# Feed-forward input of a decoder layer: the low part of every second weight tile by ACT and an accumulating DMA instead of DVE

## The chip, the core and the metric

The kernel runs on one core of a Trainium2 chip, as one launch. A core has five engines that run their own instruction queues: TensorE (PE) multiplies matrices from the on-chip memory into PSUM; VectorE (DVE), ScalarE (ACT) and GpSimd (POOL) work elementwise; SyncE (SP) here only issues DMAs. DMAs can be issued by SP, ACT or POOL, and are carried out by 16 DMA engines.

The metric is the device time of one execution in microseconds.

## What is computed

One layer of a decoder trunk on 256 tokens of 2048 features: a gated convolution branch and a block attention branch, merged and projected, then cross attention, then a gated feed-forward, each added to the residual stream, all in float32. The change is in the feed-forward input:

```python
def swiglu(h, w_in, w_out):
    g, u = jnp.split(h @ w_in, 2, axis=-1)
    return (jax.nn.silu(g) * u) @ w_out
...
    h = rmsnorm(x, norm_ffn_g[l])
    x = x + swiglu(h, w_ffn_in[l], w_ffn_out[l])
return rmsnorm(x, norm_final_g)
```

with `w_in` of 2048 x 11264 and `w_out` of 5632 x 2048.

## The kernel before

**Numbers in two parts.** TensorE gets its operands in the type float32r, which holds fewer bits than float32. To keep the precision, each operand is given as a high part (the value rounded to float32r) and a low part (the rest, value minus high part). A product then takes three matmuls into the same PSUM bank, in `mm3`: high x high (L116), high of the activations x low of the weights (L117), low x high (L118).

**The weight stream.** The whole layer is a list of blocks. A block is 1024 output columns (two ranges of 512) for both tiles of 128 tokens, over the whole contraction, in k-tiles of 128 rows. A k-tile is 128 x 1024 float32, 512 KB. Over all blocks, `stream` handles the k-tiles as one sequence with the running number q:

- `load_k` (L225) loads a k-tile into one of four `raw` buffers, from SP. In the feed-forward input the two column ranges lie apart, so that there are two DMAs, L233 and L234; in most other blocks it is one, L231.
- `split_k` (L237) makes the two parts, in one of four `whi` and one of four `wlo` buffers: ACT casts (`split`, L121), DVE subtracts (L122).
- `piece` (L258) issues the three matmuls for one token tile and one column range; a k-tile has four pieces, 12 matmuls of 512 columns.

**The order.** It is written out by the program itself, and every engine works through its own queue in that order. `ensure(q)` (L251) is called ahead of a k-tile's matmuls. It issues the splits up to tile q + 3, and ahead of each split of a tile s the loads up to tile s + 3. A buffer is taken over by the tile four numbers later: `whi` and `wlo` when TensorE has finished with them, `raw` when both the cast and the making of the low part have finished.

In the middle of a block the k-tiles are used one after the other. In its first and its last group, two k-tiles are used by turns, column range by column range (L285 to L299), and `ensure` is called once for both. At the end of a feed-forward block ACT applies SiLU (L846) and DVE multiplies (L849); the transposes of the result (L130, copied from PSUM by ACT on L133) stand among the first matmuls of the next block.

The feed-forward input is 11 blocks (`ffn_block`, L831) of 16 k-tiles. The output (`fo_block`, L875) follows it.

Of the kernel before, what the change touches and what calls it, by code (L numbers as in the profile page):

```python
# [12 lines left out]
ALU = mybir.AluOpType  # L13
# [3 lines left out]
P = 128  # L17
S = 256
D = 2048
KD = D // P  # L20
# [3 lines left out]
DFF = 5632  # L24
# [1 line left out]
EPS = 1e-6  # L26
NEG = -1e30

# columns of the packed per-partition vectors
C_MIX, C_MEM, C_CROSS, C_FFN = 0, 16, 32, 48  # L30
C_CW = 64
C_CB = C_CW + CC * TAPS
# [3 lines left out]


class Block:
    """One block of 1024 output columns for all 256 tokens: two 512-wide column
    ranges of a weight, both token tiles, the whole contraction."""  # L40

    def __init__(self, name, kt, lhs, cols, evac, before=None):
        self.name, self.kt, self.lhs, self.cols, self.evac = name, kt, lhs, cols, evac
        self.before = before


class Builder:
# [19 lines left out]
        self.ready = set()  # L67
        self.n = 0

# [1 line left out]
    def at(self, delay, fn, *args):  # L71
        heapq.heappush(self.tasks, (self.slot + delay, self.seq, fn, args))
        self.seq += 1

    def later(self, tr, n):
        """The transposes of a finished column range, a unit at a time."""
        for w in range(2):
            self.at(6 + 2 * n + 2 * w, tr, n, w)

# [31 lines left out]
        return bass.AP(tensor=src.tensor, offset=src.offset + off, ap=[[0, P], [1, n]])  # L111

    def mm3(self, out, lhs, rhs, start, stop):
        """out (+)= lhs.T @ rhs with each operand given as exact high and low parts."""
        mm = self.nc.tensor.matmul
        mm(out, lhs[0], rhs[0], start=start, stop=False)  # L116
        mm(out, lhs[0], rhs[1], start=False, stop=False)  # L117
        mm(out, lhs[1], rhs[0], start=False, stop=stop)  # L118
# [3 lines left out]
        self.nc.vector.tensor_tensor(lo, src, hi.bitcast(F32), op=ALU.subtract)  # L122

    def transposes(self, src, hi, lo, k, gain=None, mark=None):
        """Two k-tiles of both token tiles to [feature, token] and split."""
        nc = self.nc
        b = self.bank([P, 2, 2, P], "tr")
        for c in range(2):
            for t in range(2):
                nc.tensor.transpose(b[:, c, t, :], src(c, t), self.ident)  # L130
        bb = b.rearrange("p c t s -> p c (t s)")
        if lo is None:
            nc.scalar.copy(hi[:, k : k + 2, :], bb)  # L133
        elif gain is None:
            self.split(bb, hi[:, k : k + 2, :], lo[:, k : k + 2, :])
        else:
            for c in range(2):
                g = self.vecs[:, gain + k + c : gain + k + c + 1]
                nc.scalar.activation(hi[:, k + c, :], bb[:, c, :], AF.Copy, scale=g)
                nc.vector.scalar_tensor_tensor(  # L140
                    lo[:, k + c, :], bb[:, c, :], g, hi[:, k + c, :].bitcast(F32),
                    op0=ALU.mult, op1=ALU.subtract,
                )
        if mark:
            self.ready.update((mark, k + c) for c in range(2))
# [3 lines left out]
        self.nc.scalar.activation(j, src, AF.Square, accum_out=dst)  # L149

    def load_features(self, dst, src, k, n):
        """k-tiles of a [feature, token] array."""
        self.nc.sync.dma_start(dst[:, k : k + n, :], src[:, k : k + n, :])

    def split_gain(self, src, hi, lo, k, gain, mark):
        """Two k-tiles times their gains as high and low parts."""
        for i in (k, k + 1):
            g = self.vecs[:, gain + i : gain + i + 1]
            self.nc.scalar.activation(hi[:, i, :], src[:, i, :], AF.Copy, scale=g)
            self.nc.vector.scalar_tensor_tensor(  # L160
                lo[:, i, :], src[:, i, :], g, hi[:, i, :].bitcast(F32), op0=ALU.mult, op1=ALU.subtract
            )
            self.ready.add((mark, i))

    def feature_rstd(self, src, first, gap, done):
        """Reciprocal root mean square of every token of a [feature, token] tile: squares
        added over the k-tiles, then over the partitions; done(result) ends it."""
        acc = self.tok_tile([P, 2, S], "sqa")

        def square(u):  # L170
            s = self.tok_tile([P, 2, S], "sq") if u else acc
            self.nc.scalar.activation(s, src[:, 2 * u : 2 * u + 2, :], AF.Square)
            if u:
                self.nc.vector.tensor_tensor(acc, acc, s, op=ALU.add)

        def total():
            bk = self.bank([P, 2, 2], "ssq")
            for t in range(2):
                for c in range(2):
                    self.nc.tensor.matmul(bk[:, t, c : c + 1], acc[:, c, t * P : (t + 1) * P],  # L180
                                          self.ones[:, 0:1], start=True, stop=True)
            done(self.rstd_of(bk, "rf"))

        for u in range(8):
            self.at(first + gap * u, square, u)
        self.at(first + gap * 7 + 3, total)

    def rstd_of(self, ss, name):
        """[P, 2, n] partial sums of squares -> [P, 2] reciprocal root mean square."""
        nc = self.nc  # L190
        r = self.const.tile([P, 2], F32, name=self.nm(name))
        s = self.sm_tile([P, 2], "st")
        nc.vector.tensor_reduce(s, ss, axis=AX.X, op=ALU.add)
        q = self.sm_tile([P, 2], "sq")
        nc.scalar.activation(q, s, AF.Sqrt, bias=self.eps[:, 0:1], scale=1.0 / D)
        nc.vector.tensor_scalar(s, s, 1.0 / D, EPS, op0=ALU.mult, op1=ALU.add)
        nc.vector.reciprocal(r, q)
        nc.vector.tensor_tensor(s, s, r, op=ALU.mult)
        nc.vector.tensor_tensor(s, s, q, op=ALU.add)
        nc.vector.tensor_scalar_mul(s, s, 0.5)  # L200
        nc.vector.reciprocal(r, s)
        return r

# [1 line left out]
    def load_first(self):  # L205
        """The first two k-tiles, by halves in the order of their use."""
        for q in range(2):
            self.raw[q] = self.wts.tile([P, 2, 512], F32, tag="raw", name=self.nm("raw"))
        for j in range(2):
            for q in range(2):  # L210
                blk, k = self.kts[q]
                w, c = blk.cols[j]
                self.nc.sync.dma_start(self.raw[q][:, j, :], w[k * P : (k + 1) * P, c : c + 512])
# [23 lines left out]
    def split_k(self, q):  # L237
        r = self.raw.pop(q)
        hi = self.wts.tile([P, 2, 512], F32R, tag="whi", name=self.nm("whi"))
        lo = self.wts.tile([P, 2, 512], F32R, tag="wlo", name=self.nm("wlo"))  # L240
        self.split(r, hi, lo)
        self.w[q] = (hi, lo)

    def load_to(self, top):
# [71 lines left out]

        return f

# [1 line left out]
    def setup(self):  # L320
        nc, a = self.nc, self.a
        self.vecs = self.const.tile([P, NCOL], F32, name="vecs")
# [24 lines left out]
        )  # L347

    def col_tr(self, srcs, hi, lo, k, gain=None, mark=None):
        """Transposes of 256 columns from two token tiles' APs [P, 256]."""  # L350
        self.transposes(lambda c, t: srcs[t][:, c * P : (c + 1) * P], hi, lo, k, gain, mark)


# [4 lines left out]
def layer(ctx: ExitStack, tc: tile.TileContext, args, out):  # L358
# [3 lines left out]
    act, dve, pe = nc.scalar, nc.vector, nc.tensor  # L362
    b.setup()

    # ================= input norm (gain now, root mean square at evacuation) =========
    xin = b.big_tile([P, KD, S], F32, "xin")
    xh = b.big_tile([P, KD, S], F32R, "xh")
    xl = b.big_tile([P, KD, S], F32R, "xl")
# [9 lines left out]
        if q % 2 == 0 and q < 16:  # L378
            b.load_features(xin, a["x_t"], q, 2)

    # ================= input projection =================
    def bias_tile(hold, c0, c1):
        t = b.small.tile([P, 2, 512], F32, tag="bias", name=b.nm("bias"), bufs=2)
        nc.sync.dma_start(t[:, 0, :], b.bcast(a["b_in"], c0, 512))
# [48 lines left out]

        return Block(f"glu{j}", KD, b.lhs_of(xh, xl, "x"), [(a["w_in"], c0), (a["w_in"], c1)], evac, before)

    # taps per slot, alone and beside the block attention
    CONV_RATE, MOBA_RATE = 1.6, 0.6

    # causal depthwise convolution, one tap at a time, channels on partitions
    def conv_start():  # L440
        def tap(c, j):
            w = b.vecs[:, C_CW + c * TAPS + j : C_CW + c * TAPS + j + 1]
# [13 lines left out]
    ln = {}  # L456

    def tree(src, name):
        """Sum of eight [P, S] tiles."""
        s1 = b.tok_tile([P, 2, S], name)  # L460
        s2 = b.tok_tile([P, 2, S], name)
        dve.tensor_tensor(s1, src[:, 0:2, :], src[:, 2:4, :], op=ALU.add)
# [59 lines left out]
        if h == 0:  # L522
            b.at(2, ln_scale, 1)

    # keys, queries and values of the block attention
    def qk_block(name, col, which):
        hold = {}

# [88 lines left out]
        return Block(f"gate{which}{j}", KD, b.lhs_of(xh, xl, "x"),  # L617
                     [(a["w_in"], col), (a["w_in"], col + 512)], evac, before)

    # ================= merge and output projection =================  # L620
    tiles = {}

    def conv_out_block(j):
# [42 lines left out]
        return f  # L666

    def residual_block(name, w, j, kt, lhs, ssname, nxt, gain, mark, before=None):
        """x += block; sums of squares; transposed and split for the next product."""

        def evac(t, n, ps):
            c = j * 1024 + n * 512
# [21 lines left out]
        tiles["x2"] = [b.big_tile([P, KD, S], F32R, "x2") for _ in range(2)]  # L694
        tiles["ss2"] = b.const.tile([P, 2, 4], F32, name="ss2")

    # ================= cross attention =================
    def cq_block(j):
        hold = {}

# [126 lines left out]
        tiles["x3"] = [b.big_tile([P, KD, S], F32R, "x3") for _ in range(2)]  # L827
        tiles["ss3"] = b.const.tile([P, 2, 4], F32, name="ss3")

    # ================= gated feed-forward =================  # L830
    def ffn_block(j):  # L831
        hold = {}

# [24 lines left out]
            b.ready.update((("mid", k), ("mid", k + 1)))  # L858

        w = a["w_ffn_in"]  # L860
        return Block(f"ffn{j}", KD, lhs_t("x3", "x3"), [(w, 512 * j), (w, DFF + 512 * j)], evac, before)

    mids = {}

    def mid_split(j, k):
        """[P, 2, S] of the gated activations as high and low parts, ahead of use."""
        assert ("mid", k) in b.ready and ("mid", k + 1) in b.ready
        hi = b.tok_tile([P, 2, S], "mh", F32R)
        lo = b.tok_tile([P, 2, S], "ml", F32R)
# [33 lines left out]
        return Block(f"fo{j}", KF, lhs, [(w, j * 1024), (w, j * 1024 + 512)], evac, before)  # L903

    def part(t):
        """Mean square of the columns that are done, and the guard."""
        s = b.sm_tile([P, 1], "fst")
        dve.reduce_sum(s, tiles["ss4"][:, t, 0:3], axis=AX.X)
        dve.tensor_scalar(s, s, 1.0 / D, EPS, op0=ALU.mult, op1=ALU.add)
# [13 lines left out]
                dve.tensor_scalar_mul(o[:, cs], o[:, cs], q)  # L923
            (act if c == 1 else nc.sync).dma_start(rows[:, cs], o[:, cs])

    # ================= the order of the work =================
    def start():
        x_unit(0)
        for u in range(1, 8):
# [73 lines left out]
```

## Time and profile before

| | |
|---|---|
| time, median of 2 runs | 1726.76 us (1726.74 to 1726.79) |
| the profiled execution, first to last instruction | 1725.3 us |
| PE busy | 1714.2 us |
| DVE busy | 1034.3 us |
| ACT busy | 826.0 us |
| POOL busy | 1.6 us, 12 instructions |
| DMA traffic | 330.28 MB, mean 191 GB/s |
| feed-forward input, 985 to 1475 us | PE 490.0, ACT 215.5, DVE 234.9 us busy |

The profiled execution and the timed runs differ by 1.5 us, the work around the first and last instruction. Busy times are those of instructions that compute; the issue of a DMA is not counted, and stands on its own rows ("SPq" for SP's queue). A busy PE is not a PE at its peak, since matmuls are pipelined: a 512-column matmul is listed with 0.39 us, while they start 0.23 us apart. "Landing" is the time from a DMA's issue to its completion. In lists of groups, an arrow with a name after the idle time says what ended it.

### The profile page before, as it was taken

How to read it: one execution, taken by the hardware profiler on the slowest of the kernel's cores; microseconds unless marked ns; L12 is line 12 of the kernel's file. 1: busy time of each engine (PE TensorE's matmuls, PEld its weight loads, DVE VectorE, ACT ScalarE, POOL GpSimd, SP SyncE). 2: the span in 40 equal slices, each digit the busy share in tenths (PEclk: the TensorE clock that was granted, in tenths of full speed). 3: DMA queues.
4: the chain of work that ended last, by engine and by line, in shares of the span. 5: the costliest groups of instructions: out<-in, count | busy, mean ns of one | idle time of the engine just before them, and what ended most of it. 6: DMA issues, size and time to landing. Idle time of an engine off the chain costs nothing.

```text
span 1725.3 us, 20943 instructions
## 1 busy us (share of the span) xinstructions
PE 1714.2 (99%) x7830; PEld 1423.0 (82%) x7830; DVE 1034.3 (60%) x1265; ACT 826.0 (48%) x1020; POOL 1.6 (0%) x12
## 2 busy tenths in 40 slices
PE   9999999999999999999999999999999999999998
PEld 7888888888888888888888888888888888888886
DVE  6579987797765557445554554444444444555655
ACT  6544445544544556445444454444444444544543
POOL 0000000000000000000000000000000000000000
PEclk9999999999999999999999999999999999999999
DMA  8666665555665575554445555665656565655553
GB/s 297 197 205 196 195 196 172 187 191 186 208 226 181 187 244 184 184 186 155 136 158 189 184 190 191 195 195 185 193 185 193 185 194 185 216 195 193 192 193 133
DMA packets 122757, 330.28 MB, mean 191 GB/s; under 512 B 13600, under 2 KB 13728, under 8 KB 122528
## 3 DMA queue, kind: packets, MB, share of 16 engines
q1 hardware_dynamic: 122224, 328.26, 59.0%
q8 instruction: 61, 1.00, 0.2%
q10 hardware_dynamic: 432, 0.70, 0.1%
q14 instruction: 40, 0.33, 0.1%
HBM read 326.80 MB, written 2.10 MB: 191 GB/s over the span
## 4 chain that ended last, share of the span: by engine, by line
PE 99%; DMA 0%; DVE 0%; ACT 0%; DVEq 0%; issue 0%
PE acc L116 32%; PE acc L117 32%; PE acc L118 32%; PE tr L130 2%; DMA vecs<-in_vecs 0%; PE cb L118 0%; PE cs L116 0%; PE cs L118 0%; PE cs L117 0%; PE cb L117 0%; PE cb L116 0%; PE ms L570 0%; PE mo L597 0%; PE mt L589 0%; DVE wlo L122 0%; PE mo L598 0%
## 5 line engine op out<-in xcount | busy, mean ns | idle before, releaser
L122 DVE TENSOR_TENSOR wlo<-raw,whi 128x1024 fp32r<-128x1024 f32 (+1 forms) x602 | 727.7, 1220 | 563.8 <-ACT whi L121 563.0
L121 ACT CAST whi<-raw 128x1024 fp32r<-128x1024 f32 (+1 forms) x602 | 624.1, 1050 | 612.3 <-PE acc L118 525.4
L116 PE MATMUL acc<-whi,x 128*128 128x512 f32 x832 | 326.9, 393 | 0.0
L118 PE MATMUL acc<-whi,x 128*128 128x512 f32 x832 | 324.1, 390 | 0.0
L117 PE MATMUL acc<-wlo,x 128*128 128x512 f32 x832 | 323.9, 389 | 0.0
L116 PE MATMUL acc<-whi,xh 128*128 128x512 f32 x576 | 228.8, 397 | 1.0 <-ACT whi L121 1.0
L117 PE MATMUL acc<-wlo,xh 128*128 128x512 f32 x576 | 224.5, 390 | 0.2 <-DVE wlo L122 0.2
L118 PE MATMUL acc<-whi,xl 128*128 128x512 f32 x576 | 224.6, 390 | 0.0
L118 PEld LDWEIGHTS acc<-whi,x 128*128 128x128 f32 x832 | 156.2, 188 | 33.0
L117 PEld LDWEIGHTS acc<-wlo,x 128*128 128x128 f32 x832 | 156.3, 188 | 31.4
L116 PEld LDWEIGHTS acc<-whi,x 128*128 128x128 f32 x832 | 156.2, 188 | 31.4
L117 PE MATMUL acc<-wlo,mh 128*128 128x512 f32 x352 | 137.1, 389 | 0.1
L116 PE MATMUL acc<-whi,mh 128*128 128x512 f32 x352 | 137.1, 390 | 0.0
L118 PE MATMUL acc<-whi,ml 128*128 128x512 f32 x352 | 137.0, 389 | 0.0
L118 PEld LDWEIGHTS acc<-whi,xl 128*128 128x128 f32 x576 | 108.1, 188 | 23.0
L116 PEld LDWEIGHTS acc<-whi,xh 128*128 128x128 f32 x576 | 108.2, 188 | 22.7 <-ACT whi L121 1.2
L117 PEld LDWEIGHTS acc<-wlo,xh 128*128 128x128 f32 x576 | 108.3, 188 | 22.2 <-DVE wlo L122 0.8
L447 DVE SCALAR_TENSOR_TENSOR vy<-vt,vecs,vy 128x256 f32<-128x256 f32 x240 | 103.7, 477 | 0.0
L116 PE MATMUL acc<-whi,m 128*128 128x512 f32 x256 | 101.3, 396 | 0.0
L118 PE MATMUL acc<-whi,m 128*128 128x512 f32 x256 | 99.8, 390 | 0.0
L117 PE MATMUL acc<-wlo,m 128*128 128x512 f32 x256 | 99.8, 390 | 0.0
L117 PEld LDWEIGHTS acc<-wlo,mh 128*128 128x128 f32 x352 | 66.1, 188 | 14.0 <-DVE wlo L122 0.6
(206 smaller groups left out, 1630.8 us busy)
## 6 DMA issues: line engine op xcount, KB each, us to landing
raw<-in_w_ffn_in SPq DMA_DIRECT2D x352, 256.0 KB, 3.0
raw<-in_w_in SPq DMA_DIRECT2D x112, 512.0 KB, 3.6
raw<-in_w_ffn_out SPq DMA_DIRECT2D x88, 512.0 KB, 3.6
raw<-in_w_ckv SPq DMA_DIRECT2D x64, 512.0 KB, 3.6
raw<-in_w_in SPq DMA_DIRECT2D x64, 256.0 KB, 4.0
raw<-in_w_out SPq DMA_DIRECT2D x32, 512.0 KB, 4.8
raw<-in_w_cq SPq DMA_DIRECT2D x32, 512.0 KB, 4.8
raw<-in_w_co SPq DMA_DIRECT2D x32, 512.0 KB, 4.6
```

The source lines that it names most:

```text
L116: mm(out, lhs[0], rhs[0], start=start, stop=False)
L117: mm(out, lhs[0], rhs[1], start=False, stop=False)
L118: mm(out, lhs[1], rhs[0], start=False, stop=stop)
L121: self.nc.scalar.copy(hi, src)
L122: self.nc.vector.tensor_tensor(lo, src, hi.bitcast(F32), op=ALU.subtract)
L130: nc.tensor.transpose(b[:, c, t, :], src(c, t), self.ident)
L447: dve.scalar_tensor_tensor(y[:, c, :], src, w, y[:, c, :], op0=ALU.mult, op1=ALU.add)
```

## The change

The blocks of the feed-forward input get a mark, `by_dma`. For their odd k-tiles, the low part is made in another way: ACT writes the high part as before, then ACT writes the negated value into the low part's buffer, which rounds it to float32r and so gives minus the high part; then a DMA issued from POOL adds the raw tile to that buffer in place. The even k-tiles, and all other blocks, are split as before. Loads, buffers, the matmuls and their order are the same.

```diff
-    def __init__(self, name, kt, lhs, cols, evac, before=None):
+    def __init__(self, name, kt, lhs, cols, evac, before=None, by_dma=False):
         self.name, self.kt, self.lhs, self.cols, self.evac = name, kt, lhs, cols, evac
-        self.before = before
+        self.before, self.by_dma = before, by_dma
...
     def split_k(self, q):
         r = self.raw.pop(q)
         hi = self.wts.tile([P, 2, 512], F32R, tag="whi", name=self.nm("whi"))
         lo = self.wts.tile([P, 2, 512], F32R, tag="wlo", name=self.nm("wlo"))
-        self.split(r, hi, lo)
+        blk, k = self.kts[q]
+        if blk.by_dma and k % 2:
+            self.nc.scalar.copy(hi, r)
+            self.nc.scalar.mul(lo, r, -1.0)
+            self.nc.gpsimd.dma_start(lo, r, accum_op=ALU.add)
+        else:
+            self.split(r, hi, lo)
         self.w[q] = (hi, lo)
...
-        return Block(f"ffn{j}", KD, lhs_t("x3", "x3"), [(w, 512 * j), (w, DFF + 512 * j)], evac, before)
+        return Block(f"ffn{j}", KD, lhs_t("x3", "x3"), [(w, 512 * j), (w, DFF + 512 * j)], evac, before,
+                     by_dma=True)
```

The rest of the diff takes out comments and docstrings. Up to the loads (L231 to L234) the lines keep their numbers; the three new operations of the odd k-tiles stand on L243 (cast), L244 (negated copy) and L245 (accumulating DMA), and later lines move by six (SiLU from L846 to L852).

## The prediction

> **What bounds the kernel now.** I read the page's shares and its chain of waits first, then the window of the feed-forward input stage, then the timeline inside it, then the waits and the DMA landings.
>
> ```profile
> span 1725.3 us, 20943 instructions
> ...
> PE 1714.2 (99%) x7830; PEld 1423.0 (82%) x7830; DVE 1034.3 (60%) x1265; ACT 826.0 (48%) x1020; POOL 1.6 (0%) x12
> ...
> PE 99%; DMA 0%; DVE 0%; ACT 0%; DVEq 0%; issue 0%
> L122 DVE TENSOR_TENSOR wlo<-raw,whi 128x1024 fp32r<-128x1024 f32 (+1 forms) x602 | 727.7, 1220 | 563.8 <-ACT whi L121 563.0
> L121 ACT CAST whi<-raw 128x1024 fp32r<-128x1024 f32 (+1 forms) x602 | 624.1, 1050 | 612.3 <-PE acc L118 525.4
> ```
>
> The chain of waits is TensorE for 99% of the span: the program is one stream of matmuls. DVE and ACT are not busy enough to matter by themselves; both sit idle for more than 560 us ahead of these two groups, DVE until ACT's cast, and ACT mostly until TensorE gives a buffer back (L118).
>
> The window of the eleven feed-forward input blocks (columns: PE, PEld, DVE, ACT, POOL busy with counts, granted clock, DMA share, GB/s):
>
> ```profile
> 985.00:1475.00 490.00, 490.00 (x2208) 405.61 (x2207) 234.95 (x216) 215.50 (x235) 0.00 (x0) 1.00 0.60 190
> ```
>
> TensorE is busy for all of the 490 us, at full granted clock, while DVE is busy for 48% and ACT for 44%. So nothing can be won here by freeing DVE. What can be lost is decided by how much slack a weight k-tile has between its load and its first matmul. The timeline shows it: two ACT lines, one of DVE, three of SP's queue, all in mid block.
>
> ```profile
> 1043.20 1.05 ACT L121 CAST whi<-raw 128x1024 fp32r<-128x1024 f32 x1 [1.21 <-PE acc L118]
> 1045.92 1.05 ACT L121 CAST whi<-raw 128x1024 fp32r<-128x1024 f32 x1 [1.67 <-PE acc L118]
> ...
> 1044.29 1.22 DVE L122 TENSOR_TENSOR wlo<-raw,whi 128x1024 fp32r<-128x1024 f32 x1 [1.05 <-ACT whi L121]
> ...
> 1043.27 0.33 SPq L233 DMA_DIRECT2D raw<-in_w_ffn_in  x1
> 1043.64 0.43 SPq L234 DMA_DIRECT2D raw<-in_w_ffn_in  x1
> 1045.54 0.33 SPq L233 DMA_DIRECT2D raw<-in_w_ffn_in  x1
> ```
>
> The casts stand 1045.92 - 1043.20 = 2.72 us apart: that is the period of a k-tile on TensorE. The cast for tile q+3 starts when TensorE has finished tile q-1, so it is due three periods later. Its subtraction ends at 1044.29 + 1.22 = 1045.51, and 0.03 us after that SP issues the next load into the raw buffer just freed (1045.54). So each raw buffer goes round in four periods, 10.88 us: cast, subtraction, wait, load.
>
> **The change, part by part.** Of the 11 x 16 = 176 k-tiles of the stage every second, 88, changes.
>
> Removed: 88 subtractions of 1.22 us, 107 us of DVE time. What it brings is what TensorE now waits for them. The answer on line L122 gives all of it for the whole program:
>
> ```profile
> PEld acc L117: 1.4, 3
> PE acc L117: 0.2, 1
> ```
>
> 1.6 us at most, and the window above has none of it. I take 0.
>
> Added on ACT: 88 scaled copies. The trace has no copy with scale -1 of this shape; the nearest row is the cast of the same 128x1024 tile, 1.05 us, and I take that: 92 us. ACT's 215.5 us in the stage become 308 of 490. In mid block the odd tile's cast starts at T, its copy ends at T + 2.1, and the next cast, queued behind it, is due at T + 2.72: covered by 0.6 us. At a block's start the casts come in pairs and the copy would hold the PSUM copy L133 queued behind it by some 0.3 us, whose result is read only after the stage; 0.
>
> Added on POOL and the DMA engines: 88 transfers of 512 KB. POOL's queue holds nothing else (12 instructions in the program), so nobody waits behind them there. Each waits for ACT's copy. Two things then wait for its landing instead of for DVE: TensorE's L117 on that tile, and on SP's queue the L233 load that reuses the raw buffer; behind that one stand its L234 and the two loads of the next, even tile, whose buffer has been free for some time.
>
> Let A be the time from the end of ACT's copy to the landing of the accumulate. Three limits follow, each from the rows above:
>
> 1. Low part in mid block: the tile starts 3 x 2.72 = 8.16 us after its buffer was freed, about 8.0 after the cast's start, and its first L117 is a quarter of a microsecond later. A may be 8.2 - 2.1 = 6.1 us.
> 2. Raw buffer in mid block: freed at T + 2.1 + A; then SP issues two halves, 0.37 us apart, and the second lands 3.0 us after its issue (row below), 3.4 in all; the cast of the tile four further on is due at T + 10.88. A may be 10.88 - 2.1 - 3.4 = 5.4, with two semaphore steps 5.3 us. This is the one that binds.
> 3. Block edges, where two tiles are used by turns (below).
>
> ```profile
> 1025.91 1.05 ACT L121 CAST whi<-raw 128x1024 fp32r<-128x1024 f32 x1 [1.67 <-PE acc L118]
> ...
> 1031.15 0.39 PE L116 MATMUL acc<-whi,x 128*128 128x512 f32 x1
> 1031.38 0.39 PE L117 MATMUL acc<-wlo,x 128*128 128x512 f32 x1
> 1031.61 0.39 PE L118 MATMUL acc<-whi,x 128*128 128x512 f32 x1
> 1031.83 0.39 PE L116 MATMUL acc<-whi,x 128*128 128x512 f32 x1
> 1032.06 0.39 PE L117 MATMUL acc<-wlo,x 128*128 128x512 f32 x1
> ```
>
> The cast at 1025.91 is for k-tile 1 of the block that starts at 1031.15, and that tile is read already as the fourth matmul of the block, its low part at 1032.06. Tile 1 is odd. So A may be 1032.06 - 1025.91 - 2.1 = 4.05 us there, once for each of 11 blocks.
>
> Over its limit, the raw loop costs one microsecond per round of four tiles for each microsecond of A, and the stage has 176 / 4 = 44 rounds:
> loss = 44 x (A - 5.3) + 11 x (A - 4.0), each term not below 0.
> When the rounds themselves are late the edge wait is partly the same wait, so I hold the second term at its value for A = 6, 22 us, from there on.
>
> No row shows an accumulating transfer, so A is bounded by the landings of plain ones:
>
> ```profile
> raw<-in_w_ffn_in SPq DMA_DIRECT2D x352, 256.0 KB, 3.0
> ...
> raw<-in_w_ffn_out SPq DMA_DIRECT2D x88, 512.0 KB, 3.6
> ...
> raw<-in_w_cq SPq DMA_DIRECT2D x32, 512.0 KB, 4.8
> ...
> xr<-in_x SPq DMA_DIRECT2D x2, 1024.0 KB, 9.2
> ...
> gf<-in_g_final SPq DMA_DIRECT2D x1, 1024.0 KB, 6.7
> ```
>
> The lower end is 3.6 us, a plain 512 KB load. It must also read its destination, another 512 KB, so the upper end is a 1024 KB load beside the weight stream, 9.2 us. Between: going from 256 to 512 KB cost 0.6 us, so a second 512 KB should cost 1.2, which makes 4.8; the w_cq row shows that the same 512 KB can take 1.2 us more in another stage, and I allow as much for running beside the weight stream. 3.6 + 1.2 + 1.2 = 6.0 us, near the 6.7 of the 1024 KB row from the same part of the program. I take A = 6.0.
>
> Sum: 44 x 0.7 + 11 x 2.0 = 31 + 22 = 53 us. On the profiled execution, 1725.3 + 53 = 1778 us of span; the median of the runs shown, 1726.76, is 1.5 us above that span, so 1780 us. At the ends: A = 3.6 gives no loss, 1727; A = 9.2 gives 44 x 3.9 + 22 = 194, 1921.
>
> **The rivals.**
>
> *Hidden.* If the accumulate lands within 4.05 us nothing is late, and the time stays at 1727; from there to A = 5.6 the loss grows only to 13 + 18 = 31 us, 1758, still within 2%. For it: the 3.6 us row leaves 0.45 us of room, both ends of the transfer are on the chip, and POOL is empty. Against it: the second read and the weight stream. Decision point: A = 5.7, where the loss passes 2% of 1726.76, 34.5 us. The Trainium skill speaks for this rival. Its page "DMA: Bandwidth & Descriptors", section "Anatomy of one DMA — SWDGE (gpsimd) path", gives some 2.0 us plus bytes over 436 GB/s, and "Collectives: The Full Stack", Part 3, says that an add in the DMA engine costs a second source read and nothing for the add: an estimate of 2.0 + 2 x 1.2 = 4.4 us, with which the sum would be 11 x 0.4 = 4 us. No run here shows it yet; the 3.6 and 4.8 us rows leave it possible for a queue that is otherwise empty. Chance 0.32.
>
> *DMA engines full.* The stage moves 190 GB/s at a share of 0.60, which would be 317 at 1.0. The accumulates add 88 x 524,288 bytes in 490 us, 94 GB/s, or 188 if the second read counts in full: 378 GB/s. Then the stage would stretch by 378 / 317 = 1.19, 94 us, to 1821. Against it, the DMA view of the window 600 to 690 us, where loads came in a burst:
>
> ```profile
> GB/s 24 0 180 255 282 180 269 406 379 357 293 379 259 188 188 168 198 209 224 195 67 9 228 220 115 299 282 62 195 235 204 151 173 193 213 233 215 164 158 180
> ```
>
> There the engines moved up to 406 GB/s. Chance 0.10.
>
> *POOL held by DVE.* The even tiles' subtraction, 1.22 us with two operands in the same memory, runs from about T + 3.8 to T + 5.0, T being the odd tile's cast. POOL begins at T + 2.1. If its descriptor work runs into that and has to wait, A becomes 7.2: 44 x 1.9 + 22 = 106 us, 1833. The profile speaks neither for nor against, as POOL does nothing in this stage. The Trainium skill's page "SBUF — State Buffer" (the port pair that DVE and GpSimd share) has such a lock for GpSimd work that reads that memory, and not for work that only writes it; no row here shows it. Chance 0.05.
>
> *Much slower.* The transfer is done in small pieces or at the adder's own pace, so that it is over 9 us: 1912 or more. This is also how the change would fail to do what it says: a conversion in flight instead of a plain row. For it, only that no row excludes it. Chance 0.10.
>
> *Faster.* The 1.6 us above, if every wait for DVE lay in this stage, is no 2%. Chance 0.01.
>
> **How the numbers follow.** The forecast, a late raw loop with A from 5.7 to 9, has the rest, 0.42, and gives 1780. Two per cent is about what a measurement of this kernel can tell from no change. Slower: 0.42 + 0.10 + 0.05 + 0.10 = 0.67; same: 0.32; faster: 0.01. The hidden case is too likely to leave out, so the range begins at 1725, and it reaches to A of 8.7 at 1900, which leaves out the much slower case and the forecast's far end. The forecast's own range is 1762 to 1870, A from 5.7 to 8.
>
> **What would show it.** In the changed profile: ACT's second pass near 1.05 us, 88 of them; the landing of wlo<-raw from POOL near 6 us; a casting distance of more than 2.72 us in mid block, with ACT's whi waiting for the raw DMA rather than for L118; L233 on SP waiting for the accumulate; TensorE idle ahead of L117 once at each block's start, about 2 us. A landing under 4 us with TensorE still full proves the hidden case; a landing far from 6 us sizes the loss by the formula; mid-block stalls with a landing under 5 us would break the limits themselves; a DMA share near 1.0 would make it the engines.

## The result, and the profile after

The changed kernel takes 1826.12 us (median of 2 runs, 1821.21 to 1831.04) against 1726.76 us. The ratio is 1.0576, 95% interval 1.0508 to 1.0643: slower by 99 us. The forecast was 1780 us, with a range from 1725 to 1900. The profile is of the slower of the two runs, 1831.04 us; its span is 104 us longer than that of the kernel before.

From the page of the changed kernel: span, TensorE's and POOL's busy time, the chain of waits, and two rows of DMA landings (last column, us).

```profile
span 1829.3 us, 21138 instructions
...
PE 1751.6 (96%) x7830; PEld 1434.3 (78%) x7830; DVE 929.2 (51%) x1177; ACT 908.0 (50%) x1108; POOL 76.4 (4%) x100
...
PE 78%; DMA 15%; ACT 3%; issue 2%; DVE 0%; SPq 0%; ACTq 0%; DVEq 0%; POOLq 0%
...
raw<-in_w_ffn_in SPq DMA_DIRECT2D x352, 256.0 KB, 4.4
...
wlo<-raw POOLq DMA_DIRECT2D x88, 512.0 KB, 6.3
```

The feed-forward input in one window (columns as before: PE, PEld, DVE, ACT, POOL, granted clock, DMA share, GB/s):

```profile
985.00:1576.00 591.00, 524.96 (x2203) 415.28 (x2202) 130.34 (x128) 296.38 (x321) 73.82 (x87) 0.96 0.90 235
```

The last matmul of the eleven blocks ends at 1580 us instead of 1476, so that this window leaves out the stage's last 4 us. From its first matmul to its last, the stage has grown from 490 to 594 us, as much as the whole profiled execution. DVE does 105 us less in it, ACT 81 us more, and the chain, which was TensorE alone, now has DMA for 15% of the span. Who waited for the accumulates, in total, times and longest, us:

```profile
PEld acc L117: 87.2, 52
PE acc L117: 65.8, 44
```

L117 is the matmul that reads the low part. One such wait in the chain of waits, with the steps ahead of it:

```profile
1143.25 1.05 ACT whi L243
1144.30 0.96 ACT wlo L244
1145.27 0.28 issue
1145.55 6.44 DMA wlo<-raw
...
1152.03 0.50 PE acc L117
```

Cast and copy take 2.0 us, POOL starts 0.28 us later, and 6.44 us after that the transfer has landed. So A, counted from the end of ACT's copy, was 6.7 us here and, with the median landing, 0.28 + 6.3 = 6.6 us, where the forecast took 6.0.

All 2112 matmuls of the stage (11 blocks x 192) stand in the timeline. At full clock neighbours start 0.227 us apart. I took what is more than that ahead of each matmul: 0.3 us and over ahead of L117 as waiting for a low part, excesses from 0.05 to 0.3 us as a slower clock. The transposes are left out.

```
us in 11 blocks      k-tile 15   1     5     9    11   13   all    slow clock
before                    0      0     0     0     0    0     0       2.1
changed                  23.5   12.2  21.3   5.5   3.6  7.0  73.1    29.5
```

Together 73 + 27 = 100 of the 104 us that this execution lost. Three places in a block carry most of the waiting: the last k-tile of a block, the second of the next, and the sixth. Of the last column, 21 us belong to matmuls in stretches in which the granted clock was 0.50: there are 13 in the stage, 47.8 us long together. The rest are single short gaps. Of the 25 waits of 1.5 us and more, 13 have such a stretch at their end or within 2 us behind them; of the 20 shorter ones none has. TensorE's timeline at one wait on tile 5:

```profile
1165.84 0.39 PE L116 MATMUL acc<-whi,x 128*128 128x512 f32 x1
1168.00 0.50 PE L117 MATMUL acc<-wlo,x 128*128 128x512 f32 x1 [1.77 <-DMA wlo<-raw]
...
1169.04 0.63 PE L117 MATMUL acc<-wlo,x 128*128 128x512 f32 x1
1169.47 0.63 PE L118 MATMUL acc<-whi,x 128*128 128x512 f32 x1
...
1171.99 0.40 PE L118 MATMUL acc<-whi,x 128*128 128x512 f32 x1
1172.23 0.40 PE L116 MATMUL acc<-whi,x 128*128 128x512 f32 x1
```

After the wait, matmuls start 0.43 us apart (1169.04 to 1169.47) for about 3 us, while the granted clock is 0.50, and then 0.24 again.

### The profile page after: what moved, and what is told of

Its sections match the earlier page's. It is cut to its first block, busy times and chain, and to the rows that moved or that the text cites. A ratio compares the mean times of both kernels' runs of the same rounds, so it can differ in the third digit from the quotient of the medians.

```text
span 1829.3 us, 21138 instructions
## 1 busy us (share of the span) xinstructions
PE 1751.6 (96%) x7830; PEld 1434.3 (78%) x7830; DVE 929.2 (51%) x1177; ACT 908.0 (50%) x1108; POOL 76.4 (4%) x100
## 4 chain that ended last, share of the span: by engine, by line
PE 78%; DMA 15%; ACT 3%; issue 2%; DVE 0%; SPq 0%; ACTq 0%; DVEq 0%; POOLq 0%
PE acc L117 25%; PE acc L118 25%; PE acc L116 24%; DMA wlo<-raw 14%; ACT wlo L244 2%; PE tr L130 1%; ACT whi L243 1%; DMA raw<-in_w_ffn_in 1%; ACT whi L121 1%; DMA raw<-in_w_in 0%; PE cs L118 0%; PE cs L116 0%; PE cb L118 0%; PE cs L117 0%; PE cb L117 0%
## 5 line engine op out<-in xcount | busy, mean ns | idle before, releaser
L122 DVE TENSOR_TENSOR wlo<-raw,whi 128x1024 fp32r<-128x1024 f32 (+1 forms) x514 | 622.1, 1219 | 694.7 <-ACT whi L121 694.0
L121 ACT CAST whi<-raw 128x1024 fp32r<-128x1024 f32 (+1 forms) x514 | 533.6, 1048 | 484.9 <-PE acc L118 351.7
L117 PE MATMUL acc<-wlo,x 128*128 128x512 f32 x832 | 339.0, 407 | 66.0 <-DMA wlo<-raw 65.8
L116 PE MATMUL acc<-whi,x 128*128 128x512 f32 x832 | 336.5, 404 | 0.0
L118 PE MATMUL acc<-whi,x 128*128 128x512 f32 x832 | 333.2, 400 | 0.0
L117 PEld LDWEIGHTS acc<-wlo,x 128*128 128x128 f32 x832 | 161.6, 194 | 119.7 <-DMA wlo<-raw 87.2
L117 PE MATMUL acc<-wlo,xh 128*128 128x512 f32 x576 | 224.4, 390 | 0.4 <-DVE wlo L122 0.4
L118 PE MATMUL acc<-whi,xl 128*128 128x512 f32 x576 | 224.5, 390 | 0.0
L116 PEld LDWEIGHTS acc<-whi,x 128*128 128x128 f32 x832 | 161.2, 194 | 34.5
L118 PEld LDWEIGHTS acc<-whi,x 128*128 128x128 f32 x832 | 161.6, 194 | 33.5
L243 ACT CAST whi<-raw 128x1024 fp32r<-128x1024 f32 x88 | 92.5, 1051 | 129.2 <-PE acc L118 108.0
L117 PE MATMUL acc<-wlo,mh 128*128 128x512 f32 x352 | 137.1, 389 | 0.1
L118 PE MATMUL acc<-whi,ml 128*128 128x512 f32 x352 | 137.0, 389 | 0.0
L245 POOL DMA_DIRECT2D wlo<-raw x88 | 74.8, 850 | 1487.5 <-DVE xr L680 980.8
L118 PEld LDWEIGHTS acc<-whi,xl 128*128 128x128 f32 x576 | 108.1, 188 | 22.8
L117 PEld LDWEIGHTS acc<-wlo,xh 128*128 128x128 f32 x576 | 108.3, 188 | 22.6 <-DVE wlo L122 1.1
L118 PE MATMUL acc<-whi,m 128*128 128x512 f32 x256 | 99.8, 390 | 0.0
```

The source lines that it names most:

```text
L121: self.nc.scalar.copy(hi, src)
L243: self.nc.scalar.copy(hi, r)
L245: self.nc.gpsimd.dma_start(lo, r, accum_op=ALU.add)
```

## The experiments

All times are medians against runs of the kernel before on the same chip (1726.8 to 1727.3 us). Diffs are against the changed kernel. Two theories stood against each other: *latency*, that an accumulate takes longer from ACT's copy to its landing than the buffers give it; and *engines full*, that loads and accumulates together are more than the 16 DMA engines can carry in the stage's time.

**dve_add: everything but the DMA.**

```diff
-            self.nc.gpsimd.dma_start(lo, r, accum_op=ALU.add)
+            self.nc.vector.tensor_tensor(lo, r, lo.bitcast(F32), op=ALU.add)
```

> The odd k-tiles keep ACT's cast and ACT's negated copy, but DVE adds the raw tile to it, in place of the accumulating DMA. All theories that put the loss on the DMA (its landing, its share of the DMA engines) expect the time of the kernel before, 1727 us within 3. The theory that ACT's second pass holds something up in its queue expects a good part of the 99 us to stay: over 1745.

Measured: 1726.69 us, ratio 0.9998 (0.9989 to 1.0007). ACT's 88 extra passes cost nothing; the loss is all the DMA's.

**neg_first: the accumulate starts one ACT pass sooner.**

```diff
-            self.nc.scalar.copy(hi, r)
             self.nc.scalar.mul(lo, r, -1.0)
             self.nc.gpsimd.dma_start(lo, r, accum_op=ALU.add)
+            self.nc.scalar.copy(hi, r)
```

> In the odd k-tiles ACT writes the negated copy first, then POOL's DMA is issued, then ACT casts: the accumulate starts 1.05 us sooner, with the same bytes and the same number of transfers. Theory one (latency: the time from a freed buffer to the landed low part is too long, above all at block edges) expects each late place to gain up to 1 us; three such places in each of 11 blocks and part of the rounds between make 30 to 45 us, so 1780 to 1795. Theory two (the 16 DMA engines are full: 0.90 of the stage) expects no change, 1821 to 1831.

Measured: 1815.70 us, ratio 1.0498 (1.0473 to 1.0523), 10 us less than the changed kernel. That is a third of the least that latency was to give, and the two intervals (this one and 1.0508 to 1.0643) touch, so that even the 10 us are not clear of noise. The waits moved more than they shrank: on tile 15 from 23.5 to 3.7 us, on tile 1 from 12.2 to 31.1, on tile 9 from 5.5 to 18.2. A row of its waits says what had taken over:

```profile
ACT wlo L243 <- DMA raw<-in_w_ffn_in: 137.5, 37, 5.9
```

ACT's copy now waited for the raw tile, whose load waits on SP for an earlier accumulate. So this run did not tell the theories apart.

**five_buffers: five raw, high and low buffers.**

```diff
-    AHEAD = 3
-    RAW_AHEAD = 4
+    AHEAD = 4
+    RAW_AHEAD = 5
...
-        hi = self.wts.tile([P, 2, 512], F32R, tag="whi", name=self.nm("whi"))
-        lo = self.wts.tile([P, 2, 512], F32R, tag="wlo", name=self.nm("wlo"))
+        hi = self.wts.tile([P, 2, 512], F32R, tag="whi", name=self.nm("whi"), bufs=5)
+        lo = self.wts.tile([P, 2, 512], F32R, tag="wlo", name=self.nm("wlo"), bufs=5)
```

and the same for `raw`; the pool of small tiles has 6 buffers instead of 8 and that of bias tiles 1 instead of 2.

> Five raw, five high and five low buffers in place of four, loads and splits issued one tile further ahead; room for it from the pools of the small tiles (six in place of eight, and one bias tile in place of two), which may cost a few us before the feed-forward. Theory one (latency) expects the loss in the stage to go almost wholly: stage of 490 to 500 us, total under 1745. Theory two (engines full): by the packets' shares, four tiles of loads and two accumulates take 4 x 1.54 + 2 x 2.95 = 12.1 us of all 16 engines against 10.9 us of matmuls, so the stage cannot be under 530 us and the total not under 1767.

Measured: 1742.57 us, ratio 1.0090 (1.0075 to 1.0105). Its stage and its accumulates:

```profile
985.00:1475.00 490.00, 481.00 (x2146) 392.64 (x2146) 124.98 (x122) 289.97 (x314) 72.98 (x86) 1.00 1.00 273
...
wlo<-raw POOLq DMA_DIRECT2D x88, 512.0 KB, 6.8
```

Bytes go through at 273 GB/s instead of 235. The stage is 506 us long, from its first matmul to its last: a little more than the 490 to 500 that latency had, and well under the 530 that engines full had as its floor. The landing is even longer, 6.8 us, but by the same count as above TensorE waits for low parts only 12.2 us in place of 73.1, of which 8.3 on tile 15. A busy share of 1.00 is no ceiling here, and engines full falls as the cause.

**five_raw and five_parts: one kind of buffer at a time** (the same edits, for `raw` alone, and for high and low parts alone).

> Five raw buffers in place of four, loads issued one tile further ahead; high and low buffers stay four. If the raw round binds (cast, copy, accumulate, next load: 2.0 + 0.3 + 6.3 + 0.4 + 4.4 = 13.4 us for four tiles, which is just the stage's 591 / 44), a fifth buffer gives that round 2.7 us more and 40 to 80 us of the loss go: 1745 to 1785. If the low-part buffers bind (TensorE frees, cast, copy, accumulate, TensorE reads), little goes: over 1805.

> Five high and five low buffers in place of four, splits issued one tile further ahead; raw buffers stay four (one bias tile in place of two makes the room). The mirror of the run with five raw buffers: if the low-part buffers bind, 40 to 80 us of the loss go, 1745 to 1785; if the raw round binds, little goes, over 1805. If both rounds are about as long, each of the two runs alone keeps most of the loss and only both together bring the 1743 us of before.

Measured: 1812.53 us (ratio 1.0491, 1.0465 to 1.0517) and 1774.62 us (1.0268, 1.0249 to 1.0287). A raw buffer more takes off 14 us, an amount whose interval touches that of the changed kernel, high and low buffers 52, both together 84. So the low-part round is the one that binds. What ACT's cast of the odd tiles waited for in the changed kernel says the same: for TensorE, which frees the buffer of the high part, far more than for the raw tile.

```profile
ACT whi L243 <- PE acc L118: 108.0, 54, 4.8
...
ACT whi L243 <- DMA raw<-in_w_ffn_in: 17.7, 6, 6.8
```

The raw round stands close behind it: with five high and low buffers the same cast waited 50.1 us for raw tiles, and that of the even tiles 121.7.

**every_fourth, first_half, late_half: half as many accumulates, in three places.**

```diff
-        if blk.by_dma and k % 2:
+        if blk.by_dma and k % 4 == 3:
```

and `k % 2 and k < 8` (tiles 1, 3, 5, 7), `k % 2 and k > 8` (tiles 9, 11, 13, 15).

> Only every fourth k-tile (3, 7, 11, 15) goes by DMA: 44 accumulates in place of 88; the others are split by DVE. Theory two (engines full): 4 x 1.54 + 2.95 = 9.1 us of the engines for 10.9 us of matmuls, no loss, 1727 to 1732. Theory one with an unchanged landing of 6.3 us expects most of the loss to stay, since each late tile has its own buffers to wait for: 1790 to 1800; if the landing gets shorter with less traffic, to 5 us, 1737.

> Only k-tiles 1, 3, 5 and 7 of each block go by DMA: 44 accumulates as in the run with every fourth, but close together, and at the block's start, where tiles are used by turns. If traffic over the whole stage sets the landing, the time is that of every fourth, 1744. If the block edge and the local crowding set it, most of the loss stays: 1765 to 1800.

> Only k-tiles 9, 11, 13 and 15 of each block go by DMA: 44 accumulates, as close together as in the run with 1, 3, 5 and 7, so with a landing of about 6.3 us again, but in the middle and at the end of the block. If the block's first groups, where tiles are used by turns and the casts come in pairs, are where the slack is short, most of that run's 44 us goes: 1727 to 1748. If the crowding alone makes the loss, it stays: 1765 to 1780.

Measured: 1744.23 (ratio 1.0102, 1.0087 to 1.0117), 1771.58 (1.0252, 1.0234 to 1.0269) and 1769.03 us (1.0258, 1.0230 to 1.0285). Their waits by tile, and landings:

```
us in 11 blocks      tile 1    3     5     7    11    13    15    slow clock   landing
every_fourth           -      1.2    -    1.3    0.3   -   11.1      4.1         4.8
first_half            9.9     2.9  19.8   5.4    -     -     -       9.2         6.3
late_half              -       -     -     -    3.0   6.9  18.5      9.4         6.1
```

(- : not by DMA.) The same number of transfers lands in 4.8 us when they are four tiles apart and in 6.1 to 6.3 when they are two apart: what counts is the crowding at the place, not the traffic of the whole stage. The trace of first_half agrees within one run, though a long landing also overlaps more easily: the 22 accumulates that were in flight together with no other landed in 4.9 us (median), the 22 that overlapped another in 6.8. For every_fourth, 1744 us is more than the 1737 that latency gave for a landing of 5 us; most of its waiting is on tile 15. The time of late_half is the one expected of crowding alone, but two thirds of its waits are on tile 15: I had seen short slack at the start of a block only, and k-tile 15 has it too.

**plain_copy: the transfer without the addition** (`self.nc.gpsimd.dma_start(lo, r)`).

> The transfer issued by POOL copies the raw tile over the low part instead of adding to it: the addition is left out, with the second read; the same 512 KB is written, in the same order. If the second read makes the transfer long, the landing falls from 6.3 us to 4.0 to 4.8 and its share of the DMA engines by half, and the time to under 1760. If the fixed cost of such a transfer makes it long, the landing stays over 5.5 us and the time over 1790.

Measured: 1764.35 us, ratio 1.0210 (1.0195 to 1.0225). Landing, and the queue's share of the 16 engines, here and in the changed kernel:

```profile
wlo<-raw POOLq DMA_DIRECT2D x88, 512.0 KB, 4.9
...
q0 software_dynamic: 12672, 46.14, 7.4%
```

```profile
q0 software_dynamic: 12672, 46.14, 14.1%
```

Per transfer that is 0.074 x 1762.1 / 88 = 1.48 us of all engines against 0.141 x 1829.3 / 88 = 2.93: adding doubles it and makes the landing 1.4 us longer. About 62 of the 99 us hang on the addition. Landing and time came out just above what was expected of the second read (4.0 to 4.8 us, under 1760), and far from the other case.

**one_per_block: k-tile 11 alone** (`k == 11`).

> Only k-tile 11 of each block goes by DMA, 11 accumulates that never meet one another. If the other traffic makes the landing long, it falls to the shortest seen among the 88, 4.5 to 4.8 us; if it is the transfer's own, it stays near 6.3. The time is 1727 either way, as mid block allows some 6 us.

Measured: 1729.01 us, ratio 1.0008 (0.9999 to 1.0018), landing:

```profile
DMA to landing us min/median/max: 4.7/4.8/5.7
```

So an accumulate that meets no other takes 4.8 us, beside the ordinary loads, and TensorE waits for none of them. The other 1.5 us of the 6.3 come with the other accumulates: in the changed kernel 19 of the 88 overlap no other, and they landed in 5.3 us (median), the other 69 in 6.4.

**neg_five_raw and neg_five_buffers: the two edits together.**

> The negated copy first, and five raw buffers. Alone, the first took 10 us off and the second 14. If the raw round had only taken over from the low-part round in the first of them (ACT's copy waited 137 us for raw loads there), the two together give what the earlier start was expected to give, 30 us or more beyond the run with five raw buffers: 1765 to 1783. If the start of the accumulate matters little, 1800 or more.

> The negated copy first, and five buffers of all three kinds. If the 16 us that five buffers left are slack that is still short at the block edges by about a microsecond, they go: 1727 to 1733. If they are the DMA engines, busy for all of the stage there, nothing goes: 1740 to 1745.

Measured: 1814.21 us (ratio 1.0508, 1.0454 to 1.0562), a miss, and 1733.84 us (1.0044, 1.0028 to 1.0060), 9 us less than five_buffers and just above what was expected. In neg_five_raw ACT no longer waits for raw loads, yet tile 1 still loses 32.6 us. The accumulates' landing ran from 4.9 to 10.0 us, median 6.4, against 5.6 in neg_first. At one wait on tile 1 SP had issued the loads of four tiles within 4 us of the accumulate's start (two of the eight rows shown), and the chain of waits gives that accumulate 8.57 us:

```profile
1188.73 0.33 SPq L233 DMA_DIRECT2D raw<-in_w_ffn_in  x1
...
1192.56 0.42 SPq L234 DMA_DIRECT2D raw<-in_w_ffn_in  x1
...
1192.68 8.57 DMA wlo<-raw
```

Loads that a slow accumulate holds back leave together and crowd the next one. Over this run, the 28 accumulates with eight load DMAs or more issued within 4 us of their start landed in 8.5 us (median), the other 60 in 5.8. In the changed kernel the number of such loads makes no difference (6.3 us with four, 6.4 with six). No run tried this reading alone, and why the sooner start is worth so little with four low buffers stays open.

No version beats the kernel before: its stage has no idle TensorE to win.

## Why the prediction was right in direction and short in size

**Nothing to gain on DVE, nothing lost on ACT: right.** dve_add shows both terms at 0.

**A = 6.0 us: a little short.** 0.28 + 6.3 = 6.6. The 4.8 for a transfer with its second read, worked out from the load rows, is what the lone one took. But that one ran beside the weight stream, for which the forecast allowed 1.2 us more; the 1.5 us that came instead are the accumulates' own crowding, which it did not have. That the two are nearly equal is luck.

**The limits: the binding one was wrong.** The prediction had the raw round bind, with A up to 5.3 us, and sized mid block at 31 us by it. five_raw and five_parts show the low-part buffers binding. Of the prediction's signs, SP's L233 did wait for the accumulate (232.5 us in all), but ACT's cast waited for L118 and not for the raw tile. With the measured 6.6 the formula would give 44 x 1.3 + 22 = 79 us, 57 of them in raw rounds that did not bind: that the sum came within a factor of two of 99 is partly luck. Tiles 9 to 13 lost 16.1 us. For this the limit of 6.1 us on the low part in mid block is the right one to hold against 6.6.

**The edge term: the step that was too small.** It named one place per block, k-tile 1, and priced it at 22 us. There are three, and they lost 57 us. The two that were missed can be read from the timeline of before. K-tile 15 is in the last group, where two tiles are used by turns just as in the first, so its low part, too, is read only 1071.11 - 1064.96 = 6.15 us after the start of its cast: A up to 4.05.

```profile
1064.96 1.05 ACT L121 CAST whi<-raw 128x1024 fp32r<-128x1024 f32 x1 [1.67 <-PE acc L118]
...
1071.11 0.39 PE L117 MATMUL acc<-wlo,x 128*128 128x512 f32 x1
```

For k-tile 5, ACT's casts come in a pair behind the PSUM copy:

```profile
1037.71 2.00 ACT L121 CAST whi<-raw 128x1024 fp32r<-128x1024 f32 x2
```

The second, tile 5's, starts at about 1038.7, its copy would end at 1040.7, and its low part is read 1031.15 + 5 x 2.72 + 0.88 (two sets of transposes) + 0.23 = 1045.9: A up to 5.2. With A = 6.6 tile 15 should wait 2.5 us and tile 5 1.4; they waited 23.5 / 11 = 2.1 and 21.3 / 11 = 1.9. Tile 1 waited 1.1 instead of 2.5, because its cast is issued ahead of tile 15's wait and gains from it: after the three waits of over 2 us on tile 15 that another block of the stage followed, the next tile 1 did not wait at all.

**The clock: missing.** About 21 us are matmuls at half speed, which the sum did not have. The granted clock of the stage fell from 1.00 to 0.96, and came back to 1.00 in five_buffers, where no wait reached 1.5 us.

**The rivals.** Hidden: a lone transfer took 4.8 us and was hidden in mid block (one_per_block). With 88 in the stage, which crowd one another and also stand where the slack is short, it was not. The 4.8 us are near the 4.4 us estimated from the Trainium skill's two pages. The doubled engine time agrees with what the Trainium skill's page "Collectives: The Full Stack", Part 3, says of the second source read. Engines full: the share did reach 0.90, and this rival's 1821 us is nearer to the result than the forecast is. But its stage of 490 x 1.19 = 583 us, for all the bytes, took 506 in five_buffers, so that the number was right for another reason. POOL held by DVE: its busy time per accumulate was 0.84 to 0.99 us over all 88, leaving no room for a hold of 1.22 us in that stretch. Much slower, and faster, did not occur.

## What to carry to other kernels

When a step on a busy engine is replaced by a DMA, ask how long the new chain is from the freed buffer to the use, and compare it with the slack at each place of the program, not in mid block alone: wherever tiles are used by turns or prepared in pairs, the slack is shorter, and such places should be counted one by one. Take the transfer's price beside the traffic that it will have, other such transfers above all. A TensorE that waits even for 2 us can then pay again with a slower clock; here about half of such waits did.

## What the runs showed of the hardware

- An accumulating transfer of 512 KB within the on-chip memory, issued by POOL, landed in 4.8 us when alone among the weight loads and in 6.3 with 88 in the stage; a plain one in 4.9 with 88. By its packets' time it holds the 16 engines for 2.9 us, a plain one for 1.5.
- After a wait of 1.9 us (1166.07, when the next matmul was due, to 1168.00) matmuls ran for about 3 us at 0.43 us instead of 0.23, at a granted clock of 0.50. The changed kernel has 13 such stretches, and no wait under 1.5 us was followed by one. The Trainium skill's page "TensorE: Matmul & The Clock Gate", Part 1, has such a halving, with an idle window of some 3.4 us ahead of it; here a shorter wait was enough, though not each time.
- A DMA share of 1.00 over the stage (five_buffers, 273 GB/s) is not the engines' limit: in neg_five_buffers the share of the same window is 1.02, at 277 GB/s. Loads only took longer to land, 5.4 us in five_buffers against 3.0 before.
